# First MLP matrix of a decoder block: squared quarter held on chip, the order of its activation sums, and their layout in memory

## The chip, the cores and the metric

The kernel runs on one core of a Trainium2 chip. The metric is the device time of one execution in microseconds (us), as the median of several runs. Engines are called PE (TensorE), DVE (VectorE), ACT (ScalarE), POOL (GpSimd) and SP (SyncE); the latter two only issue DMAs in the parts that matter here. PSUM is the matmuls' accumulator memory, SBUF the on-chip memory with 128 partitions.

## The reference

A single decoder block in fp32 on 512 tokens of width 2048: RMSNorm, a gated mix of a short convolution and a forgetting attention, a projection back, then an RMSNorm and an MLP with a squared ReLU, and a final RMSNorm. The part that the change touches is the MLP:

```python
h = rmsnorm(x, g_mlp)              # 512 x 2048
u = jnp.square(jax.nn.relu(h @ w_ff1))   # w_ff1 2048 x 8192
x = x + u @ w_ff2                  # w_ff2 8192 x 2048
```

## The kernel before, in words

**Matrix products.** All large products are done in 2 x 2 blocks by a scheme with seven products in place of eight (A11, A12, S4, S2, S3, S1, A22). For each, sums and differences of blocks are formed on both sides: "weight sums" of quarters of w, and "sums of activations". Each fp32 operand is split into a high part that PE multiplies directly (type fp32r) and a low part, the difference: `split` (L99 to L102) writes th on ACT (L101) and tl on DVE (L102). A product is three passes, high by high, high by low, low by high.

**The first MLP matrix** has 16 groups of 512 columns of w_ff1, each one object of the class Group (L166). A group loads four quarters of 1 MB, x00, x10, x01, x11, on SP's queue (L174 to L181), each into a buffer that a done quarter has released (`free`). `head` (L216) runs the products A11 and A12 and hands the quarter (0,0) of the result to `put`; `tail` (L232) runs S4, S2, S3, S1, hands over (1,1) and (0,1), then runs A22 and hands over (1,0). Each product has 48 matmuls of 128 x 256 here. Weight sums are `sub` (L105), four a group; the sums of results are `add` (L108); `snap` (L194) copies a finished accumulator out of PSUM into a small tile o. One product's th and tl have two buffers each.

**After the matrix.** `put_u` (L809 to L847) receives a quarter, applies ReLU in place (L836), squares it (L813), and when both quarters of a column half j are there, forms the seven sums of activations that the second matrix will need: `sums(j)` (L815 to L833) writes them to a tile r of 7 x 256 values per partition, copies the high part to rh (ACT, L829), leaves the low part in r (DVE, L830), and stores both to the DRAM array s_d on POOL's queue (L832 and L833). There is one buffer for r and one for rh. Quarter (0,0) comes long before its partner (1,0), so it is squared at once, stored to the DRAM array c_d (L839, on POOL's queue), and read back into r (L818) when sums(0) is formed.

`sums(0)` is not called at once: `put` appends it to the list `later`, which the next group's `tail` drains after the S4 product (L241). `sums(1)` is called directly by the put of quarter (0,1); quarter (1,0), which completes sums(0), is the last of a group.

**What sets the order.** Engines run their instructions in order, each waiting on semaphores. Tile pools decide when a buffer may be written again: the next r waits until the store of the last one has landed. The framework lays out each engine's order from the written order and may set an instruction ahead of one that it does not depend on.

**The second MLP matrix** goes through w_ff2 in 8 segments. `load_sums` reads the sums of a segment from s_d into tiles us (L872 to L881), three tiles of two sums each and one of a single sum, on POOL's queue; `unit` (L929) loads quarters y of w_ff2 on SP's queue and runs the seven products. The first tile is requested in the last group of the first matrix, the other three behind it. s_d holds, for each partition, seven sums, and in each two parts (high, low), four row blocks and 256 values, so one store writes runs of 256 values (1 KB) that lie 8 KB apart.

Of the kernel before, what the change touches and what calls it, by code (L numbers as in the profile page):

```python
# [8 lines left out]
F32 = mybir.dt.float32  # L9
F32R = mybir.dt.float32r  # L10
BF16 = mybir.dt.bfloat16
AF = mybir.ActivationFunctionType
# [3 lines left out]
P = 128  # L16
S = 512
# [3 lines left out]
HS = S // 2  # L21
# [4 lines left out]
DFF = 4 * D  # L26
# [19 lines left out]
def tile_hybrid_block(ctx: ExitStack, tc, x, g_mix, w_in, b_f, b_gate, conv_w, w_conv_out,  # L46
                      w_attn_out, w_mix_out, g_mlp, w_ff1, w_ff2, g_final, out):
    nc = tc.nc
    x, out = x[0], out[0]
# [5 lines left out]
    main = ctx.enter_context(tc.tile_pool(name="main", bufs=1))  # L55
    pp = ExitStack()
    psum = pp.enter_context(tc.tile_pool(name="psum", bufs=1, space=bass.MemoryType.PSUM, reuse_waits="tile"))
    dram = ctx.enter_context(tc.tile_pool(name="dram", bufs=1, space=bass.MemoryType.DRAM))

    def phase(name):  # L60
        return tc.tile_pool(name=name, bufs=1, reuse_waits="tile")
# [16 lines left out]
    y_d = dram.tile([CT, P, S], F32, name="y_d")  # L78
    a_d = dram.tile([CT, P, S], F32, name="a_d")
    x1_d = dram.tile([NT, P, D], F32, name="x1_d")  # L80
    c_d = [dram.tile([P, 2, HS], F32, name=f"c_d{i}") for i in range(DFF // S)]
    s_d = [dram.tile([P, 7, 2, 4, HS], F32, name=f"s_d{i}") for i in range(DFF // 1024)]


    warm = const.tile([P, 1], F32, name="warm")
# [18 lines left out]
    def sub(out, a, b):  # L104
        nc.vector.tensor_tensor(out=out, in0=a, in1=b, op=ALU.subtract)  # L105

    def add(out, a, b):
        nc.vector.tensor_tensor(out=out, in0=a, in1=b, op=ALU.add)  # L108
# [50 lines left out]
    def moving(t):  # L159

        return lambda q: (t[:, 0, q, :], t[:, 1, q, :])


    free, later = [0, 1, 2, 3], []

    class Group:  # L166
# [65 lines left out]
        def tail(self):  # L232
            if self.at:
                X = self.X
            else:
                X = {(i, 0): self.load(i, 0) for i in range(2)}
            X[0, 1], X[1, 1] = self.load(0, 1), self.load(1, 1)
            a = self.a
            c = self.acc("c")
            self.run(c, "S4", X[1, 1], True)  # L240
            while later:  # L241
                later.pop(0)()
            sub(X[0, 0], X[0, 1], X[0, 0])
            sub(X[0, 1], X[1, 1], X[0, 1])
            sub(X[1, 1], X[1, 1], X[0, 0])
            self.run(a, "S2", X[1, 1], False)
            sub(X[1, 0], X[1, 0], X[1, 1])
            self.done(1, 1)
            s2 = self.snap(a)
            d = self.acc("d")  # L250
            self.run(d, "S3", X[0, 1], True)
            self.done(0, 1)
            d1 = self.snap(d, self.scale)
            self.run(a, "S1", X[0, 0], False)
            self.done(0, 0)
            s4 = self.snap(a, self.scale)
            add(d1, d1, s4)
            self.put(1, 1, d1)
            self.plus(s4, c, self.scale)
            self.put(0, 1, s4)  # L260
            self.run(d, "A22", X[1, 0], False)
            self.done(1, 0)
            self.plus(s2, d)
            self.put(1, 0, s2)
# [55 lines left out]
    def rstd_of(part):  # L320
        v = stat.tile([P, 1], F32, tag="v", name="v")
        nc.vector.tensor_reduce(out=v, in_=part, axis=AX.X, op=ALU.add)
        r = stat.tile([P, 1], F32, tag="r", name="r")
        nc.gpsimd.tensor_tensor(out=r, in0=v, in1=mhalf, op=ALU.pow)
        return r
# [64 lines left out]
    for t in range(NT):  # L390
        h = xp[t // 2][:, t % 2]
        n = 4 if t == 0 else 2
# [182 lines left out]
    n = 0  # L575
# [45 lines left out]
    for c in range(4):  # L621
        held = main.tile([P, 4, S], F32, tag="x1", name="held")
# [183 lines left out]

    def put_u(g):  # L809
        quarters = {}  # L810

        def square(v, out):
            nc.scalar.activation(out=out, in_=v, func=AF.Square)  # L813

        def sums(j):  # L815
            r = pf.tile([P, 7, HS], F32, tag="r", name="r")
            if j == 0:
                nc.gpsimd.dma_start(out=r[:, 0:6:5], in_=c_d[g])  # L818
            else:
                square(quarters[0, j], r[:, 0:6:5])  # L820
            low = quarters[1, j]
            square(low[:, 1, :], r[:, 3, :])
            square(low[:, 0, :], low[:, 0, :])
            add(r[:, 4, :], low[:, 0, :], r[:, 3, :])
            sub(r[:, 1, :], r[:, 0, :], low[:, 0, :])
            sub(r[:, 2, :], r[:, 4, :], r[:, 0, :])
            sub(r[:, 6, :], r[:, 5, :], r[:, 2, :])
            h = pf.tile([P, 7, HS], F32R, tag="rh", name="rh")
            nc.scalar.activation(out=h, in_=r, func=AF.Copy)  # L829
            nc.vector.tensor_tensor(out=r, in0=r, in1=h.bitcast(F32), op=ALU.subtract)  # L830
            q = 2 * (g % 2) + j
            nc.gpsimd.dma_start(out=s_d[g // 2][:, :, 0, q, :], in_=h.bitcast(F32))  # L832
            nc.gpsimd.dma_start(out=s_d[g // 2][:, :, 1, q, :], in_=r)  # L833

        def put(i, j, v):
            nc.scalar.activation(out=v, in_=v, func=AF.Relu, scale=common)  # L836
            if (i, j) == (0, 0):
                square(v, v)
                nc.gpsimd.dma_start(out=c_d[g], in_=v)  # L839
                return  # L840
            quarters[i, j] = v
            if j == 0:
                later.append(lambda: sums(0))
            elif len(quarters) == 2:
                sums(1)

        return put  # L847

    def ff1(g, banks):
        return Group(w_ff1, g * S, g * S + HS, HS, Q2.moving, mm_cols, banks, put_u(g))  # L850
# [3 lines left out]
    pf = ph.enter_context(phase("pf"))  # L854
    n = turns[0] + 1
# [16 lines left out]
    def load_sums(seg, ks, ST):  # L872

        for k in ks:
            place, names = US[k]
            t = main.tile([P, 2, 2, 4, HS], F32R, tag=f"t{place}", name="us")
            nc.gpsimd.dma_start(out=t[:, :len(names)].bitcast(F32), in_=s_d[seg][:, 2 * k:2 * k + len(names)])
            for e, n in enumerate(names):
                ST[n] = moving(t[:, e])

    for g in range(2, DFF // S):  # L881
        group = ff1(g, ((2 + 2 * (g % 2),), (3,), (1,), (7,)))
        group.head(True)
        if g == DFF // S - 1:
            us0 = {}
            load_sums(0, (0,), us0)
        group.tail()

    load_sums(0, (1, 2, 3), us0)
    later.pop()()  # L890
    ph.close()
# [105 lines left out]
    for seg in range(NSEG):  # L997
        ST = us0
        if seg > 0:
            ST = {}  # L1000
            load_sums(seg, range(4), ST)
        if seg == 1:
            gf = pg.tile([P, D], F32, tag="h", name="gf")
            nc.gpsimd.dma_start(out=gf, in_=g_final.partition_broadcast(P))
        for cg in range(2):
            unit(seg, cg, ST)

    for t in (2, 3, 0, 1):
        r = rstd_of(ss3[:, t, :])
# [43 lines left out]
```

## Time and profile before

| | us |
|---|---|
| median of 3 runs | 2546.12 |
| lowest, highest | 2540.99, 2546.52 |
| profiled execution, its time | 2549.66 |
| span of its records | 2547.8 |
| busy: PE, DVE, ACT, POOL | 2469.5, 1904.8, 1144.5, 128.2 |
| mean granted TensorE clock | 0.992 |
| first matrix, 1249 to 1900: PE, DVE, ACT busy of 651 | 620.6, 537.2, 371.7 |
| second matrix, 1900 to 2548: PE, DVE, ACT busy of 648 | 622.6, 526.3, 243.1 |
| 1 MB load of w_ff1, median from issue to landing | 8.4 |
| 896 KB store of rh, of r | 6.4, 7.8 |
| 2 MB load of us | 10.0 |

"Busy" is the time in which an engine executed. A line of the waits names the engine and the line of code that waited, then what released it, then the total, the number of waits and the longest. The chain of waits follows the last instruction back from releaser to releaser. The clock of a stretch is a share of TensorE's full rate.

### The profile page before, as it was taken

To read this page: it belongs to the slowest core of one execution; us is meant where nothing else is said; L and a number is where in the kernel's file an instruction comes from. 1 tells how busy PE (TensorE), PEld (TensorE's weight loads), DVE (VectorE), ACT (ScalarE), POOL (GpSimd) and SP (SyncE) were. 2 spreads that over 40 slices of the span, in tenths; PEclk is the share of its full clock that TensorE was granted. 3 is DMA by queue.
4 is the path that set the end of the run, shared out by engine and by line. 5 is a ranking of instruction groups with operands and counts; after the bars stand their busy time and mean duration, and the time that the engine had idled before them with its cause. 6 is when DMAs were issued, how large, how long until landed. Compare 5 with 4: busy or idle time off the path is not lost.

```text
span 2547.8 us, 39010 instructions
## 1 busy us (share of the span) xinstructions
PE 2469.5 (97%) x16895; PEld 2269.4 (89%) x16895; DVE 1904.8 (75%) x1498; ACT 1144.5 (45%) x1120; POOL 128.2 (5%) x184
## 2 busy tenths in 40 slices
PE   8999999999999999999989999999999999999997
PEld 7999899999999988888889999999998887787785
DVE  7877677779767734435778888888887878878888
ACT  6433443344444622235545655655654333333343
POOL 0000000000000000000001111111111000000000
PEclk9999999999999999999999999999999999999998
DMA  7554444466443544436565665757587556654573
GB/s 240 158 186 153 155 137 129 133 195 210 138 150 115 199 159 143 136 118 231 167 199 182 216 218 189 246 171 236 193 299 286 181 210 219 226 194 162 191 256 106
DMA packets 287871, 473.45 MB, mean 186 GB/s; under 512 B 10236, under 2 KB 194644, under 8 KB 283476
## 3 DMA queue, kind: packets, MB, share of 16 engines
q1 hardware_dynamic: 260704, 330.40, 40.6%
q0 software_dynamic: 26128, 139.47, 14.7%
q8 instruction: 132, 2.16, 0.3%
q10 hardware_dynamic: 868, 1.10, 0.1%
q14 instruction: 39, 0.32, 0.0%
HBM read 374.46 MB, written 96.47 MB: 185 GB/s over the span
## 4 chain that ended last, share of the span: by engine, by line
PE 49%; DVE 12%; DMA 10%; issue 6%; ACT 4%; POOL 1%; POOLq 0%; ACTq 0%; SPq 0%; DVEq 0%
DMA s_d<-r 5%; DVE tl L102 5%; DMA x<-in_w_ff_dram 4%; ACT th L101 4%; PE a L137 3%; PE a L139 3%; PE a L141 3%; PE a L154 3%; PE a L155 2%; PE a L157 2%; PE pt L295 2%; PE pn L304 2%; PE pn L302 2%; PE pt L297 2%; PE pn L303 2%
## 5 line engine op out<-in xcount | busy, mean ns | idle before, releaser
L102 DVE TENSOR_TENSOR tl<-x,th 128x2048 fp32r<-128x2048 f32 (+1 forms) x252 | 576.0, 2289 | 215.0 <-ACT th L101 199.9
L101 ACT ACTIVATE th<-x 128x2048 fp32r<-128x2048 f32 (+1 forms) x252 | 481.8, 1916 | 474.1 <-PE a L139 164.2
L105 DVE TENSOR_TENSOR x<-x,x 128x2048 f32<-128x2048 f32 (+1 forms) x144 | 329.3, 2287 | 32.5 <-DMA x<-in_w_ff_dram 24.8
L101 ACT ACTIVATE th<-y 128x2048 fp32r<-128x2048 f32 x80 | 153.6, 1921 | 270.2 <-DVE y L105 102.9
L102 DVE TENSOR_TENSOR tl<-y,th 128x2048 fp32r<-128x2048 f32 x80 | 182.8, 2285 | 43.6 <-ACT th L101 43.6
L137 PE MATMUL a<-ST,th 128*128 128x256 f32 x768 | 186.1, 286 | 22.6 <-ACT th L101 19.7
L154 PE MATMUL a<-th,us 128*128 128x512 f32 x512 | 201.7, 394 | 4.4 <-ACT o L836 3.4
L102 DVE TENSOR_TENSOR tl<-raw,th 128x2048 fp32r<-128x2048 f32 x40 | 91.7, 2293 | 150.7 <-ACT th L101 150.2
L155 PE MATMUL a<-th,us 128*128 128x512 f32 x512 | 200.1, 391 | 0.0
L139 PE MATMUL a<-ST,th 128*128 128x256 f32 x768 | 184.4, 283 | 0.0
L137 PEld LDWEIGHTS a<-ST,th 128*128 128x128 f32 x768 | 149.7, 195 | 25.4 <-ACT th L101 22.3
L101 ACT ACTIVATE th<-raw 128x2048 fp32r<-128x2048 f32 x40 | 76.7, 1918 | 176.7 <-PE pt L296 71.5
L139 PEld LDWEIGHTS a<-ST,th 128*128 128x128 f32 x768 | 149.7, 195 | 0.0
L137 PE MATMUL a<-S,th 128*128 128x256 f32 x576 | 136.2, 280 | 4.3 <-ACT th L101 4.2
L157 PE MATMUL a<-tl,us 128*128 128x512 f32 x512 | 136.8, 389 | 0.1
L139 PE MATMUL a<-S,th 128*128 128x256 f32 x576 | 135.6, 279 | 0.0
L154 PEld LDWEIGHTS a<-th,us 128*128 128x128 f32 x512 | 96.6, 189 | 29.6 <-ACT th L101 6.2
L137 PE MATMUL d<-ST,th 128*128 128x256 f32 x512 | 118.1, 277 | 1.0 <-ACT o L194 1.0
L139 PE MATMUL d<-ST,th 128*128 128x256 f32 x512 | 118.0, 276 | 0.0
L155 PEld LDWEIGHTS a<-th,us 128*128 128x128 f32 x512 | 96.7, 189 | 19.7
L157 PEld LDWEIGHTS a<-tl,us 128*128 128x128 f32 x512 | 96.0, 188 | 20.4 <-DVE tl L102 0.5
L137 PEld LDWEIGHTS a<-S,th 128*128 128x128 f32 x576 | 108.5, 188 | 5.6 <-ACT th L101 5.3
(276 smaller groups left out, 6257.8 us busy)
## 6 DMA issues: line engine op xcount, KB each, us to landing
x<-in_w_in_dram SPq DMA_DIRECT2D x86, 1024.0 KB, 5.8
x<-in_w_ff_dram SPq DMA_DIRECT2D x66, 1024.0 KB, 8.4
y<-in_w_ff_dram SPq DMA_DIRECT2D x64, 1024.0 KB, 6.2
us<-s_d POOLq DMA_DIRECT2D x24, 2048.0 KB, 10.0
s_d<-rh POOLq DMA_DIRECT2D x32, 896.0 KB, 6.4
s_d<-r POOLq DMA_DIRECT2D x32, 896.0 KB, 7.8
raw<-in_w_mix_out_dram SPq DMA_DIRECT2D x24, 1024.0 KB, 5.1
g_d<-o SPq DMA_DIRECT2D x32, 256.0 KB, 2.2
```

The costliest lines, as they stand in the source:

```text
L101: nc.scalar.activation(out=hi, in_=src, func=AF.Copy)
L102: nc.vector.tensor_tensor(out=lo, in0=src, in1=hi.bitcast(F32), op=ALU.subtract)
L105: nc.vector.tensor_tensor(out=out, in0=a, in1=b, op=ALU.subtract)
L137: nc.tensor.matmul(o, hi[:, q, js], Sh, start=first and q == 0 and j == 0, stop=False, skip_group_check=True)
L139: nc.tensor.matmul(o, hi[:, q, js], Sl, start=False, stop=False, skip_group_check=True)
L141: nc.tensor.matmul(o, lo[:, q, js], Sh, start=False, stop=q == nq - 1, skip_group_check=True)
L154: nc.tensor.matmul(o, Sh, hi[:, q, :], start=begin and q == 0, stop=False, skip_group_check=True)
L155: nc.tensor.matmul(o, Sl, hi[:, q, :], start=False, stop=False, skip_group_check=True)
L157: nc.tensor.matmul(o, Sh, lo[:, q, :], start=False, stop=q == nq - 1, skip_group_check=True)
L295: nc.tensor.matmul(ps[j], hi[:, q, js], xh, start=k == 0, stop=False)
L297: nc.tensor.matmul(ps[j], lo[:, q, js], xh, start=False, stop=k == kt - 1)
L302: nc.tensor.matmul(ps, xh, hi, start=first, stop=False)
```

## The change

Three things in the first matrix, and one line on a bank:

1. c_d is gone. `hold` squares quarter (0,0) into an on-chip tile c (one buffer, 2 KB per partition); sums(0) copies it into r on ACT. `hold` itself goes through `later`.
2. `later` is drained behind the snapshot that follows the S2 product, not behind S4, so that the written order has the weight sums first.
3. s_d has the seven sums innermost: one store writes one run of 7 x 256 values (7 KB) per partition. A tile us is then read in two DMAs (high and low), in runs of two sums, 2 KB (1 KB for the tile with one sum).
4. In the last group the accumulator c of S4 lies in bank 2 and not in bank 1.

```diff
-    c_d = [dram.tile([P, 2, HS], F32, name=f"c_d{i}") for i in range(DFF // S)]
-    s_d = [dram.tile([P, 7, 2, 4, HS], F32, name=f"s_d{i}") for i in range(DFF // 1024)]
+    s_d = [dram.tile([P, 2, 4, 7, HS], F32, name=f"s_d{i}") for i in range(DFF // 1024)]
...
             self.run(c, "S4", X[1, 1], True)
-            while later:
-                later.pop(0)()
             sub(X[0, 0], X[0, 1], X[0, 0])
...
             s2 = self.snap(a)
+            while later:
+                later.pop(0)()
...
+    held = []
...
             if j == 0:
-                nc.gpsimd.dma_start(out=r[:, 0:6:5], in_=c_d[g])
+                nc.scalar.activation(out=r[:, 0:6:5], in_=held.pop(0), func=AF.Copy)
...
-            nc.gpsimd.dma_start(out=s_d[g // 2][:, :, 0, q, :], in_=h.bitcast(F32))
-            nc.gpsimd.dma_start(out=s_d[g // 2][:, :, 1, q, :], in_=r)
+            nc.gpsimd.dma_start(out=s_d[g // 2][:, 0, q], in_=h.bitcast(F32))
+            nc.gpsimd.dma_start(out=s_d[g // 2][:, 1, q], in_=r)
+
+        def hold():
+            c = pf.tile([P, 2, HS], F32, tag="c", name="c")
+            square(quarters[0, 0], c)
+            held.append(c)
 
         def put(i, j, v):
             nc.scalar.activation(out=v, in_=v, func=AF.Relu, scale=common)
+            quarters[i, j] = v
             if (i, j) == (0, 0):
-                square(v, v)
-                nc.gpsimd.dma_start(out=c_d[g], in_=v)
-                return
-            quarters[i, j] = v
-            if j == 0:
+                later.append(hold)
+            elif j == 0:
                 later.append(lambda: sums(0))
-            elif len(quarters) == 2:
+            elif (0, 1) in quarters and (1, 1) in quarters:
                 sums(1)
...
-            t = main.tile([P, 2, 2, 4, HS], F32R, tag=f"t{place}", name="us")
-            nc.gpsimd.dma_start(out=t[:, :len(names)].bitcast(F32), in_=s_d[seg][:, 2 * k:2 * k + len(names)])
+            t = main.tile([P, 2, 4, len(names), HS], F32R, tag=f"t{place}", name="us")
+            for e in range(2):
+                nc.gpsimd.dma_start(out=t[:, e].bitcast(F32), in_=s_d[seg][:, e, :, 2 * k:2 * k + len(names)])
...
-        group = ff1(g, ((2 + 2 * (g % 2),), (3,), (1,), (7,)))
+        group = ff1(g, ((2 + 2 * (g % 2),), (3,), (1 if g < DFF // S - 1 else 2,), (7,)))
```

More of the change, by code (lines that the diff above doesn't have):

```diff
@@ L875, in load_sums @@
             place, names = US[k]
-            t = main.tile([P, 2, 2, 4, HS], F32R, tag=f"t{place}", name="us")
-            nc.gpsimd.dma_start(out=t[:, :len(names)].bitcast(F32), in_=s_d[seg][:, 2 * k:2 * k + len(names)])
+            t = main.tile([P, 2, 4, len(names), HS], F32R, tag=f"t{place}", name="us")
+            for e in range(2):
+                nc.gpsimd.dma_start(out=t[:, e].bitcast(F32), in_=s_d[seg][:, e, :, 2 * k:2 * k + len(names)])
             for e, n in enumerate(names):
-                ST[n] = moving(t[:, e])
+                ST[n] = moving(t[:, :, :, e])
     for g in range(2, DFF // S):
-        group = ff1(g, ((2 + 2 * (g % 2),), (3,), (1,), (7,)))
+        group = ff1(g, ((2 + 2 * (g % 2),), (3,), (1 if g < DFF // S - 1 else 2,), (7,)))
         group.head(True)
```

## The prediction

> **What bounds the kernel now.** I read the page first, then the waits of each engine in the stage of the first MLP matrix, then the chain of waits of one group, then the DMA view of the same stretch.
>
> ```profile
> PE 2469.5 (97%) x16895; PEld 2269.4 (89%) x16895; DVE 1904.8 (75%) x1498; ACT 1144.5 (45%) x1120; POOL 128.2 (5%) x184
> ```
>
> TensorE is nearly always busy, so the change can only win what PE loses now. The table by stage gives for this stage, 1249 to 1900 us of the span:
>
> ```profile
> 1249.00:1900.00 651.00, 620.64 (x5330) 616.88 (x5328) 537.20 (x402) 371.74 (x365) 79.01 (x96) 0.98 0.63 209
> ```
>
> PE is idle 651.0 − 620.6 = 30.4 us there, and runs at a clock of 0.98. For 13 steady groups (1345.8 to 1870.6, each from its S4 product to the next) the period is 524.8 / 13 = 40.37 us. The matmuls of this stage follow each other at 0.1133 us, so a group's 7 × 48 = 336 need 38.08 us. The excess is 2.29 us a group, 29.8 us in all: 17.5 idle (the same table gives 507.3 busy of 524.8), and 12.3 in which PE is busy but slow. Two slices of that table around one stall say where the slow part is from:
>
> ```profile
> 1431.50:1434.40 2.90, 0.82 (x7) 0.63 (x7) 2.90 (x3) 2.13 (x2) 0.00 (x0) 1.00 0.95 325
> 1434.40:1437.80 3.40, 3.40 (x17) 3.40 (x18) 3.11 (x3) 3.24 (x4) 1.29 (x2) 0.50 0.23 65
> ```
>
> A gap of 2.9 − 0.8 = 2.1 us, then 3.4 us at clock 0.50: half of it, 1.7 us, is lost. A larger stall so costs itself and 1.7 us. (The Trainium skill, "TensorE: Matmul & The Clock Gate", Part 1, asks for no PE gaps over some 3.4 us; by that none of these stalls, at most 3.2 us in the steady groups, would halve the clock, and removing them would be worth 17.5 us, not 29.8, and the 21.7 us below would be some 13. The 0.50 behind a gap of 2.1 us speaks against that reading, so the trace's figure stands.)
>
> What makes PE stall, from the waits of all engines in the same stretch:
>
> ```profile
> POOL r L818 <- DMA s_d<-r: 67.7, 14, 6.0
> ACT th L101 <- DVE x L105: 61.2, 14, 4.6
> ...
> ACT r L813 <- DMA s_d<-r: 36.2, 16, 6.5
> ...
> DVE x L105 <- DMA x<-in_w_ff_dram: 24.8, 14, 3.9
> ...
> PE a L137 <- ACT th L101: 19.7, 13, 2.8
> ...
> DVE r L105 <- DMA r<-c_d: 12.1, 6, 4.9
> ```
>
> PE waits once a group (13 times) for th of S2. ACT's th waits for the weight sums on DVE, and DVE for x. The chain of one group names the transfers behind it:
>
> ```profile
> 1671.73 6.32 DMA s_d<-r
> ...
> 1678.33 0.72 POOL r L818
> ...
> 1688.84 11.83 DMA s_d<-r
> ...
> 1700.76 0.07 ACT r L813
> ```
>
> A loop closes on itself. Means of groups 1 to 13, from the timeline: S2's start to the end of tl of S1 (call it T0) 10.0 us; T0 releases the buffer for x01, which lands 11.9 us later, and the store of sums(0) is issued 2.2 us after T0 and lands 13.1 us after it. The next tl of A12 can start 3.8 us after x01 or 2.65 us after that landing, whichever is later (a sum on DVE lies ahead of it, and ACT has r, L813, ahead of its th): 16.4 us after T0. From there DVE and ACT run without a gap to the next S2, 13.9 us. 10.0 + 16.4 + 13.9 = 40.3, the period measured.
>
> **The change, part by part.** *c_d goes.* Per group a 256 KB store and a 256 KB load vanish from POOL's queue, 0.52 MB, 1.4 us of the DMA engines at the 375 GB/s that they reach while crowded, and at a bad place: between T0's predecessors and the loads of x. The r add (L105) no longer waits for c_d: 12.1 us in 6 groups. ACT gets a copy of 128x512 instead, 0.62 us by the square of the same shape (L813), 16 times. It stands ahead of th of S1, where ACT waits about 1 us for PE now, and S1's product starts only some 4 us later, so I cost it at nothing; if that cover is gone it is 16 × 0.62 = 10 us at most.
>
> *The sums move behind tl of S3.* In the built order PE and SP are unchanged. On DVE one add per group moves behind tl of S3; the sums stay ahead of tl of S1. On ACT th of S3 no longer stands behind r (L813), which waits 36.2 us in 16 cases for the store's landing; the copy out of c now meets that wait. Behind it in ACT's queue are r<-o, c<-o, th of S1, rh and the snapshot. In the group at 1677 the landing came at 1678.05 and th of S1 began at 1681.27, held by PE; with 1.66 us of small work in between, 1.6 us of slack stays. Together with c_d I take the first leg from 10.0 to 9.0 us: groups in which c_d was not late show 8.2 to 9.3 now. Bounds: 0 (DVE is late anyway) and −1.8.
>
> *Seven sums in a row.* Each store goes as rows of 7 KB, not 1 KB. In 1693 to 1696 us a store of r crosses a load of x:
>
> ```profile
> q0 software_dynamic: 240, 0.93, 82.3%
> q1 hardware_dynamic: 210, 0.21, 20.7%
> ```
>
> Equal numbers of packets, so the queues alternate packet by packet: 0.823 × 16 × 3 / 240 = 165 ns for 3.9 KB of the store, 47 ns for 1 KB of x. A line through both gives an estimate of 292 ns for 7 KB. A 896 KB store is then 8 packets per DMA engine, 2.3 us, instead of 15, 2.4 us, and lets 7 fewer packets of x through. Two stores: 14 × 47 ns = 0.66 us of x that come behind, not between. So the store lands up to 0.66 + 1.4 us sooner, I take 1.5; x01 is 1.4 sooner for c_d and up to 0.66 later for this, I take 0.75. The second leg's later end gains 1.1: 16.4 to 15.3. Bounds: −2.1, and +0.7 if the rows give no relief and c_d none.
>
> The loop is then 9.0 + 15.3 + 13.9 = 38.2, beside the 38.08 of PE. As legs scatter by about 1 us, and a late group cannot be made up, I take 38.7: 13 × (40.37 − 38.7) = **21.7 us**.
>
> *The first groups.* The longest wait for c_d, 4.9 us, is there: r waits until 1320.5, the store of r is issued at 1326.2 and lands at 1335.9, ACT waits for it, and PE stalls 1.0 and 3.3 us (d, and b L137 <- ACT th L101) with a half-clock stretch behind. Without c_d that store leaves some 4 us sooner. Of 1.0 + 3.3 + 1.7 = 6.0 I take **5 us**.
>
> *Reads for the second matrix.* us is read in 64 DMAs of 2 KB runs, not 32 of 16 KB runs; the total is the same and first use lies 15 us or more behind it, except at the start, where y10's load (21.3 us) runs beside 16 KB packets of 611 ns and costs about 0.6 us of PE. Bounds −1.5 (that stall and a sooner landing) and +3 (a late us at the start, whose k=1 tile has about 2 us to spare); I take **−0.9**. The bank of the last group changes nothing: that first product waits for another bank.
>
> Sum: 21.7 + 5 + 0.9 = 27.6 us of the profiled run's 2549.66 (its span is 2547.8): 2522.1. That run is 3.5 us above the median shown, 2546.12; on the median's scale it is 2518.6. I predict 2520. All excess of these parts gone, 29.8 + 6 + 1.5 = 37.3, gives 2509.
>
> **Rivals.** (a) *Only the wait for c_d goes.* x01 and the stores land no sooner, because stores and loads of x fill the DMA engines anyway (99% busy in slices). For it: x00 and x10 are what c_d collides with, x01 is issued later. Against: c_d<-o landed only at 1686.63, when T0's loads start. Loop 39.3, say 39.5 with scatter: 13 × 0.87 + 5 = 16 us, **2532**. (b) *c_d was covered.* 12.1 us of wait in 6 groups are also taken up by DVE being ahead; the late landing then moves to tl of A12 unchanged: **2543**, within 0.2%. The change also does less than it says on DVE: the sums still precede tl of S1. (c) *Slower: long packets starve x.* With 292 ns against 47, x01 and x11 get 14% of a DMA engine while a store runs, 22% before. If the stores are queued deep ahead of x01, x01 lands after T0 + 13.5 rather than 11.9 and the weight sum on DVE becomes the later end of the second leg; from there every us adds to the period. At 1 us a group it is 13 × 1.0, and 1.7 in some four groups more for the clock: about 20 us, less the 5 at the start: **2561**. Against it: only 0.66 us can be displaced by my count, and c_d's 1.4 us go. (The Trainium skill, "DMA: Bandwidth & Descriptors", Queues, rings and completion order, says that each engine goes round its queues a whole packet at a time; the equal counts above agree.)
>
> **Chances.** Forecast (2509 to 2529) 0.60; (a) 0.17; (b) 0.09; (c) 0.14. About 0.2%, 5 us, is what a measurement of this kernel can tell from no change. Faster 0.77, same 0.09, slower 0.14. The range for 8 in 10 takes the forecast, (a), and the edge of (b): 2508 to 2545.
>
> **What would show it.** No DVE wait for c_d; PE's waits for th of S2 down from 19.7 to under 8 us; period near 38.7; the clock of the stage at 0.99; x01 landing about 11 us after its issue and the store of sums(0) under 12 us after T0; POOL's store issue to landing no longer than now; the b stall of 3.3 us gone. Wrong, if x01 takes longer than 12 us, if ACT waits for s_d before th of S1 and PE's a then waits at S1, or if y and us delay the second matrix by more than 1 us.

## The result and the profile after

The changed kernel takes 2523.35 us in the median of 6 runs (2512.57 to 2533.48), the kernel before 2546.32 (2533.48 to 2551.06). The ratio is 0.9913, with a 95% interval of 0.9891 to 0.9935: 23 us faster, 2520 was forecast. The profiled execution of after took 2533.48 us (span 2531.8), 16.2 less than that of before. Three stages, each from its first matmul to that of the next (the first from the span's start):

| us | before | after | difference |
|---|---|---|---|
| ahead of the first MLP matrix | 1242.3 | 1245.2 | +2.9 |
| first MLP matrix | 660.0 | 643.9 | −16.1 |
| second MLP matrix, to the last matmul | 632.3 | 629.4 | −2.9 |

The first row holds nothing that the change touches; what it shows comes below. The page of after, its engines and the chain that ended last:

```profile
PE 2477.9 (98%) x16895; PEld 2281.2 (90%) x16895; DVE 1901.8 (75%) x1498; ACT 1153.8 (46%) x1136; POOL 112.5 (4%) x184
...
PE 69%; DVE 8%; ACT 3%; DMA 1%; issue 1%; POOL 0%; ACTq 0%; POOLq 0%; SPq 0%; DVEq 0%
```

DMA had been 10% of the chain and DVE 12%; PE is 69% of it now, 49% before. The row of the table by stage for 1249 to 1900 us:

```profile
1249.00:1900.00 651.00, 641.02 (x5402) 637.66 (x5401) 548.72 (x414) 391.42 (x392) 40.27 (x71) 1.00 0.60 205
```

PE is idle 10.0 us in place of 30.4. Its waits in that stretch, all of them, and then three lines from the list of all engines:

```profile
PE a L136 <- ACT th L100: 7.1, 3, 2.7
PE c L136 <- ACT th L100: 1.6, 1, 1.6
PE a L153 <- ACT o L842: 1.2, 1, 1.2
```

```profile
DVE x L104 <- DMA x<-in_w_ff_dram: 5.0, 4, 2.5
...
ACT rh L830 <- DVE r L104: 4.7, 14, 0.7
...
ACT r L814 <- DMA s_d<-r: 4.2, 1, 4.2
```

The 13 waits for th of S2 (in 13 of the 16 groups) are down to 3, all in the first groups. b's stall of 3.3 us is gone, DVE waits 5.0 us for x (24.8 before) and never for c_d, ACT's r waits once. So the loop that the prediction describes no longer holds PE up. Yet the period of the 13 steady groups is 39.78 us, 0.59 less than before, not the 1.67 that was forecast: 12 of them take 39.57 us, without one stall. The matmuls themselves are further apart. The same 35 us of the span in before, another stretch of before, and the first in after (columns: length, PE busy with its number of matmuls, PEld, DVE, ACT, POOL, clock, DMA share, GB/s):

```profile
1476.00:1511.00 35.00, 35.00 (x312) 35.00 (x311) 28.52 (x23) 19.43 (x19) 4.53 (x6) 1.00 0.62 207
1353.00:1388.00 35.00, 35.00 (x299) 35.00 (x298) 27.53 (x23) 20.94 (x22) 3.69 (x5) 1.00 0.58 190
```

```profile
1476.00:1511.00 35.00, 35.00 (x300) 35.00 (x298) 30.22 (x21) 21.52 (x23) 2.13 (x4) 1.00 0.54 194
```

PE is busy throughout and the clock is 1.00 in all three, but 312 matmuls start in the first and 299 or 300 in the others. From start to start it is 113.3 ns or 117.8 ns, with no value between, for a whole stretch: 336 of them make 38.08 or 39.57 us. Before has both, after the slow one from 1350.8 us for 537 us on end. In the 13 steady groups 353 of before's 4368 intervals are slow, and 4319 of after's: against 113.3 ns throughout that is 1.6 us in before and 19.2 in after. This is not in the prediction, and the experiments had to separate it from the loop.

### The profile page after: what moved, and what is told of

The parts are those of the page before. It is cut to its first block, busy times and chain, and to the rows that moved or that the text cites. A ratio compares the mean times of both kernels' runs of the same rounds, so it can differ in the third digit from the quotient of the medians.

```text
span 2531.8 us, 38985 instructions
## 1 busy us (share of the span) xinstructions
PE 2477.9 (98%) x16895; PEld 2281.2 (90%) x16895; DVE 1901.8 (75%) x1498; ACT 1153.8 (46%) x1136; POOL 112.5 (4%) x184
## 4 chain that ended last, share of the span: by engine, by line
PE 69%; DVE 8%; ACT 3%; DMA 1%; issue 1%; POOL 0%; ACTq 0%; POOLq 0%; SPq 0%; DVEq 0%
PE a L136 6%; PE a L138 6%; PE a L140 6%; PE d L138 4%; PE d L136 4%; PE d L140 4%; PE a L153 3%; PE a L154 2%; PE a L156 2%; ACT th L100 2%; DVE tl L101 2%; PE pt L295 2%; PE pt L296 2%; PE pn L302 2%; PE pn L301 2%; PE pn L303 2%
## 5 line engine op out<-in xcount | busy, mean ns | idle before, releaser
L104 DVE TENSOR_TENSOR x<-x,x 128x2048 f32<-128x2048 f32 (+1 forms) x144 | 329.0, 2285 | 11.7 <-DMA x<-in_w_in_dram 6.1
L136 PEld LDWEIGHTS a<-ST,th 128*128 128x128 f32 x768 | 146.3, 190 | 7.7 <-ACT th L100 7.7
L138 PEld LDWEIGHTS a<-ST,th 128*128 128x128 f32 x768 | 146.2, 190 | 0.0
L138 PE MATMUL d<-ST,th 128*128 128x256 f32 x512 | 121.6, 280 | 0.0
L136 PE MATMUL d<-ST,th 128*128 128x256 f32 x512 | 121.6, 280 | 0.0
L156 PEld LDWEIGHTS a<-tl,us 128*128 128x128 f32 x512 | 96.0, 188 | 20.7 <-DVE tl L101 0.9
```

The source lines that it names most:

```text
L136: nc.tensor.matmul(o, hi[:, q, js], Sh, start=first and q == 0 and j == 0, stop=False, skip_group_check=True)
L138: nc.tensor.matmul(o, hi[:, q, js], Sl, start=False, stop=False, skip_group_check=True)
L156: nc.tensor.matmul(o, Sh, lo[:, q, :], start=False, stop=q == nq - 1, skip_group_check=True)
```

## The experiments

Theory: two limits, the loop (forecast at 38.2 us after the change) and PE at one of two spacings. Rivals: the loop is itself 39.57; or the slow spacing is what PE gives without rest. The times of kernels run together share their runs of before.

**The edits by themselves.** hold_only, rows_only and order_only are before with one part of the diff each; hold_order is after with the old layout of s_d.

```diff
hold_only:  -  r[:, 0:6:5] <- DMA of c_d[g]
            +  r[:, 0:6:5] <- copy of held.pop(0); hold() appended to later
rows_only:  -  s_d tile [P, 7, 2, 4, HS]
            +  s_d tile [P, 2, 4, 7, HS]; us read in two DMAs
order_only: -  later drained behind run(c, "S4")
            +  later drained behind s2 = self.snap(a)
```

> Before, with c_d replaced by the on-chip tile c alone (sums still drained behind S4, old layout of s_d). First theory (the loop through c_d, x01 and the store sets the period): no wait of DVE for c_d, first leg about 9.5 instead of 10.0 us, x01 about 0.7 us sooner; PE idle in the 13 steady groups falls from 17.5 to about 8 us, the first groups win 5 us; about -13 us. Rival (c_d was covered): idle stays at 15 to 18 us, time within 0.2%. Cadence theory, found in the trace of after: matmuls of 256 columns follow each other at 113.3 or at 117.8 ns, and keep the one they have until PE next pauses, so a group without a stall takes 38.08 or 39.57 us; the stretches of this kernel show only these two values, and a change of value only behind a pause.

> Before, with the new layout of s_d alone (stores in rows of 7 KB, us read in 64 DMAs; c_d stays). First theory: the store of sums(0) lands 0.5 to 1 us sooner after T0, x01 up to 0.4 us later; PE idle in the steady groups 12 to 17 us; -3 to -6 us in all. Rival (long packets starve x): x01 lands later than 12.5 us after T0, idle rises above 20 us and the time by 10 us or more. Cadence theory: stalls remain, so both cadences appear, with a change behind a stall only.

> Before, with the list of postponed sums drained behind the snapshot of S2 alone (c_d and the old layout stay). First theory: DVE still waits for c_d, th of S3 no longer stands behind the r that waits for the store's landing; first leg 9.6 us, PE idle of the steady groups 14 to 17 us, -2 to -5 us. Rival (it does nothing, since the sums still precede tl of S1): within 0.2%, idle 17 to 18 us.

> After without the new layout of s_d (and without the moved bank): c on chip and the sums drained behind S2. First theory: PE idle of the steady groups about 4 to 6 us, so a period of 38.5 at the quick cadence, and -18 us in all; the difference to after is what the rows of 7 KB bring. Rival (the rows are what matters): idle above 12 us. Cadence theory: where the stalls are gone the period is 38.08 or 39.57, one of them over many groups, and its time lies apart from another run of the same kernel by up to 13 x 1.49 = 19 us for this stage alone.

| | median, us | ratio to before (95%) | first matrix, us | stalls in 13 groups, us | period, us |
|---|---|---|---|---|---|
| before | 2549.5 | 1 | 660.0 | 19.6 | 40.38 |
| hold_only | 2524.63 | 0.9916 (0.9883 to 0.9949) | 643.2 | 2.2 | 39.73 |
| rows_only | 2530.94 | 0.9927 (0.9899 to 0.9954) | 645.8 | 2.9 | 39.78 |
| order_only | 2545.75 | 0.9986 (0.9964 to 1.0008) | 662.1 | 21.8 | 40.44 |
| hold_order | 2530.85 | 0.9917 (0.9887 to 0.9947) | 642.0 | 5.6 | 39.56 |

(The last three columns are of the profiled executions, that of before as in the first table; a stall is what a gap of over 0.3 us between starts of matmuls has beyond one interval. Kernels run later had runs of before of their own, 2545.9 and 2542.31 us in the median, and their ratios go by these.) c on chip and the rows of 7 KB each bring as much as the whole change, and the order brings nothing that can be measured. My figures for single edits failed, for hold_only by size (−13 us expected, −25 in the medians), for rows_only (−3 to −6 expected, −19) by far, and for order_only (−2 to −5 expected), whose interval includes no change. But both kernels show the same picture as after: one stall, then 39.57 us in every group. In hold_order the two limits are seen side by side. Its groups 3 to 6 are at the quick spacing and stall by 0.63, 1.00, 0.96 and 0.43 us; behind the last of these PE goes on at the slow spacing, and the other groups take 39.57 us with no stall. So that loop is about 39 us by these stalls, too long for 38.08 and short enough for 39.57. In order_only DVE still waits for c_d, and PE for th of S2 (from all waits):

```profile
PE a L137 <- ACT th L101: 17.1, 14, 2.3
DVE r L105 <- DMA r<-c_d: 15.6, 7, 4.6
```

**Disturbing the spacing.** One matmul of a product is issued as two of half the columns:

```diff
-   nc.tensor.matmul(o, hi[:, q, js], Sl, start=False, ...)
+   for cs in halves(q, j):   # two slices of 128 columns at q == 4, j == 0
+       nc.tensor.matmul(o[:, cs], hi[:, q, js], Sl[:, cs], start=False, ...)
```

halves7 does it in every 256-column product, halves1 in every seventh, both on after.

> After, with one of the 48 matmuls of every 256-column product issued as two of 128 columns (same sums, same result), so PE's stream is disturbed once a product without any wait. Cadence theory: the disturbance lets the spacing of the matmuls be drawn anew 7 times a group, as a stall does, so both 113.3 and 117.8 ns appear in the stretch from 1350 to 1860 us, changes fall on the split matmuls, and the mean of the steady groups lies between 38.1 and 39.6 us with no 500 us stretch of one value; two halves cost at most 0.01 to 0.1 us more than one whole, 0.1 to 0.7 us a group. Rival 1 (the slow value is what PE gives without rest, whatever the alignment): 117.8 ns throughout, time as after or up to 9 us longer. Rival 2 (halves are dear): period over 40 us.

> The same with one split matmul in every seventh 256-column product only (once a group of the first MLP matrix). Cadence theory: one chance a group to change the spacing; stalls left a quick stretch behind them in some 3 of 4 cases, so the steady groups last 38.1 to 38.6 us after a quick draw and 39.6 after a slow one, the mean over runs 5 to 10 us below after. Rival 1 (rest, not alignment): 117.8 ns throughout, time as after.

halves1 took 2508.7 us (2502.3 to 2509.36), ratio to before 0.9862 (0.983 to 0.9894); halves7 took 2543.49, ratio 1.0005 (0.9985 to 1.0026). At the split the timeline of PE in halves1 reads (start, duration with its overlap, operation, shape, count):

```profile
1383.85 0.33 PE L145 MATMUL a<-ST,th 128*128 128x128 f32 x2
1384.02 0.33 PE L142 MATMUL a<-ST,th 128*128 128x256 f32 x1
1384.19 0.28 PE L145 MATMUL a<-ST,th 128*128 128x256 f32 x1
```

From the start of the first half to that of the second whole matmul behind is 0.34 us, three times 113 ns: the split costs one more interval, 0.113 us. And it does more than draw anew, which the cadence theory had not expected. I count, from 480 to 1915 us, what lies between one stretch of at least 10 matmuls at one spacing and the next. In the five kernels that split every seventh product, a split with no stretch at half clock beside it led from the slow spacing to the quick one in 20 of 20 cases, and from the quick one it never left it (103 of 103). A pause without a split or half clock (13 kernels, all but halves7) led from quick to slow in 40 of 113 cases, from slow to quick in 17 of 34. So all steady groups of halves1 but the first run at 38.21 us without a stall, and the spread of its runs shrinks from 21 us to 7; the median is 15 us below after, where 5 to 10 were expected. The rival of "rest" falls: 0.1 us without any wait is enough. halves7 is at the quick spacing too, but has 204 more splits, 23 of the 35 us by which it is slower; the other 12 us (7 ahead of the first matrix, 5 behind it) were not followed up.

The stage ahead of the first matrix, 480 to 880 us, has the same 256-column products: 400 us of after at the slow spacing, and in hold_only quick. The same 60 us in after and in hold_only:

```profile
700.00:760.00 60.00, 60.00 (x512) 60.00 (x511) 40.38 (x22) 27.33 (x26) 0.00 (x0) 1.00 0.44 132
```

```profile
700.00:760.00 60.00, 60.00 (x531) 60.00 (x531) 39.33 (x22) 28.77 (x29) 0.00 (x0) 1.00 0.53 162
```

It is why the first row of the first table moves by itself: 1245.2 us in after, 1229.0 in hold_only. Before ran a fifth of these matmuls (675 intervals) at the quick spacing, which is the 3 us by which its first row is shorter than after's.

**How long is the loop after the change?** more_dve adds 1.26 us of DVE work to every group of after; hold_rows is after without the moved drain and bank.

```diff
more_dve:  -  sub(r[:, 6, :], r[:, 5, :], r[:, 2, :])
           +  the same four times for j == 0
```

> After, with the last of the sums(0) formed four times instead of once (1.26 us more on DVE in every group, ahead of tl of S1; the result is the same). Cadence theory: at the slow spacing PE needs 39.57 us a group and the loop through DVE and the loads is shorter, about 38.2 to 38.7 us, so the loop becomes 39.5 to 40 and costs at most 0 to 6 us in 13 groups. Rival (39.57 is the loop itself, the new period is set by DVE and the transfers): 13 x 1.26 = 16 us more and a stall in every group.

> After without the moved drain and the moved bank (c on chip, rows of 7 KB, sums drained behind S4). First theory, as amended by the single edits (each of c on chip and rows of 7 KB alone already brings the loop below the 39.57 us that PE needs at the slow spacing): no stalls in the slow stretches, time equal to after within the scatter of single runs, 2515 to 2535 us. Rival (the order matters once the other two are there): stalls at S2 of 0.5 us or more in most groups and 5 us more than after.

more_dve took 2526.17 us, ratio 0.9916 (0.9885 to 0.9948); its profiled execution fell on the quick spacing (that of after on the slow one), and

```profile
1476.00:1511.00 35.00, 35.00 (x312) 35.00 (x311) 31.95 (x27) 20.97 (x22) 1.60 (x3) 1.00 0.57 205
```

it runs 12 groups on end at 38.08 us (one of them 38.19) without a stall, 1.26 us notwithstanding. Not all of the 1.26 us is in the loop's way: in halves1 DVE has 0.28 us to wait in front of this tl, and the shortest first legs (S2 to T0) are 9.2 us in more_dve and 8.2 in halves1. So the loop of after is at most 38.08 − 1.0 = 37.1 us, shorter than the 38.2 forecast and than my 38.2 to 38.7 in the expectation, and 39.57 was PE, not the loop. The rival falls. hold_rows took 2515.16 us, ratio 0.9899 (0.9867 to 0.9931), first matrix 643.8 us, as after (643.9): the order adds nothing there either.

**The parts with the spacing held.** The split of halves1 in before, and in before with one or two parts of the change:

> Before, with the split matmul in every seventh 256-column product, which holds the spacing of the matmuls at 113.3 ns, so that stalls alone are left. Amended theory (two limits: a loop of about 40.3 us through c_d, the stores and x01, and PE's 38.08 or 39.57): the loop binds, so the first MLP matrix stays within 5 us of before (653 us from its first to the last matmul) with a period of 40 us; only the stage ahead of it, 480 to 880 us, gains up to 15 us. Rival (the spacing alone was the change's gain): the first MLP matrix drops below 640 us.

> The tile c on chip in place of c_d alone, at the quick spacing. Amended theory: the loop without c_d is about 39 us (hold_order showed stalls of 0.6 to 1.0 us in its quick groups), above 38.2: stalls of 0.5 to 1 us in most groups, first MLP matrix 620 to 633 us. Rival (c_d was the whole loop): no stalls, as halves1.

> The rows of 7 KB alone, c_d kept, at the quick spacing. Amended theory: the loop is below 39.57 us (rows_only had no stall at the slow spacing) but above 38.2, so stalls of 0.3 to 1 us in most groups, first MLP matrix 620 to 633 us, and DVE still waits for c_d. Rival (the rows are the whole gain): no stalls in the steady groups, as halves1.

> Both, without the moved drain and bank, at the quick spacing. Amended theory: the loop is about 37 us, below PE's 38.2; no stalls, first MLP matrix within 3 us of halves1, so the moved drain brings nothing that counts. Rival (the order is needed): stalls of 0.3 us or more in most groups.

| with the split | median, us | ratio to before (95%) | first matrix | stalls in 13 groups | period |
|---|---|---|---|---|---|
| before | 2536.96 | 0.9967 (0.9945 to 0.999) | 656.9 | 20.3 | 40.30 |
| c on chip | 2518.62 | 0.989 (0.9856 to 0.9924) | 638.9 | 12.2 | 39.41 |
| rows of 7 KB | 2519.18 | 0.9891 (0.9858 to 0.9924) | 638.9 | 6.1 | 39.03 |
| both | 2507.89 | 0.9843 (0.9806 to 0.988) | 628.6 | 3.2 | 38.49 |
| all (halves1) | 2508.7 | 0.9862 (0.983 to 0.9894) | 627.0 | 2.4 | 38.43 |

Here the parts add in good part: in the first matrix each brings 18 us and both together 28, where PE's floor cuts them off; at the slow spacing one part alone had brought as much as all. The split alone leaves before's first matrix where it was, so the loop bound there, and moves the time by the stage ahead. The first matrix came out at 638.9 where 620 to 633 was expected of either part: the stalls of the first groups remain. PE's waits for th of S2 in before, with c on chip, with the rows, and with both, all with the split:

```profile
PE a L143 <- ACT th L101: 19.5, 10, 2.9
```

```profile
PE a L142 <- ACT th L100: 15.6, 14, 2.9
```

```profile
PE a L143 <- ACT th L101: 8.1, 7, 2.8
```

```profile
PE a L142 <- ACT th L100: 4.9, 3, 2.7
```

The legs of the loop, means of groups 1 to 13 as in the prediction (x01, store and tl of A12 count from T0):

| us | S2 to T0 | x01 lands | store lands | tl of A12 | then to S2 |
|---|---|---|---|---|---|
| before | 10.0 | 11.7 | 13.1 | 16.3 | 14.0 |
| before with the split (before_halves) | 9.7 | 11.5 | 13.2 | 16.2 | 14.2 |
| c on chip (hold_halves) | 8.9 | 12.2 | 13.6 | 16.5 | 13.9 |
| rows (rows_halves) | 8.9 | 11.7 | 11.1 | 15.7 | 14.3 |
| all (halves1) | 8.2 | 11.0 | 11.1 | 15.1 | 14.9, PE's turn |

c on chip shortens the first leg only. The rows shorten both: the store lands 2.1 us sooner, x01 becomes the later end of the second leg, and DVE's waits for c_d fall from 8.4 to 4.8 us. That these fall because a store that lands sooner lets the read of c_d start sooner is argued, not shown. The store itself is faster where no load runs beside it, in the issues of the DMA view, 1710.9 to 1718.6 us of before and 1698.6 to 1704.9 us of after:

```profile
s_d<-rh POOLq DMA_DIRECT2D x1, 896.0 KB, 4.7
s_d<-r POOLq DMA_DIRECT2D x1, 896.0 KB, 5.3
```

```profile
s_d<-rh POOLq DMA_DIRECT2D x1, 896.0 KB, 3.9
s_d<-r POOLq DMA_DIRECT2D x1, 896.0 KB, 3.9
```

These are typical: 30 such stores of after have a median of 3.9 us, 29 of before one of 5.3. Beside loads (13 stores of rh in each) the larger difference is at the start: from the issue to the first packet it takes 4.6 us in the median of before, 2.7 in hold_only, 1.1 in rows_only and in after. The store of r behind it then lands 13.2 us after the issue of rh in before and 11.9 in rows_only and after, so most of that head start is lost again on the way.

And packets beside a load, with a store under way all the time (after, 1682.5 to 1684.5 us):

```profile
q0 software_dynamic: 101, 0.72, 85.8%
q1 hardware_dynamic: 112, 0.10, 17.3%
```

## Why the prediction came out, point by point

**The bound.** Right: the loop held PE, and it was the loop that the change shortened. The floor beneath it was the step that failed: "a group's 7 × 48 = 336 need 38.08 us". That is one of two values. The rows of before already had the other, 299 matmuls in 35 us at clock 1.00, and I put all of the slow busy time down to the clock. For before that was nearly right: of its excess of 29.8 us, 19.6 are stalls, 8.1 half clock and 1.6 the slow spacing. For after it was not: 19.2 of its 22.2 us are the slow spacing.

**First leg, 10.0 to 9.0.** Right in kind; 8.9 by c on chip alone, 8.2 in all. The copy on ACT shows no cost, as forecast. The moved sums were given a share of it and have none that shows: order_only is 0.9986 (0.9964 to 1.0008), and hold_rows equals after. The rows were given none and have one: 8.9 by the rows alone.

**Second leg, 16.4 to 15.3.** Measured 15.1, but the parts are not those of the sum. The 1.4 us of traffic that c_d takes away brought x01 and the store nothing by itself (12.2 and 13.6 us with c on chip, 11.5 and 13.2 before, all with the split): of this, rival (a) was right. On top of the rows it goes with an x01 that lands 0.7 us sooner (11.0 against 11.7). The rows alone brought the store forward by 2.1 us, where 0.66 was the most that I allowed them. I had priced a store by the time of its packets, 2.3 against 2.4 us of the DMA engines. Alone the packets take 279 ns for 7 KB and 189 ns for 4 KB, 2.23 against 2.65 us a store, and I left out what lies ahead of them: POOL's issue (0.53 in place of 0.94 us) and the wait for the first packet.

**Long packets starve x.** Rival (c) did not come in the time, though its mechanism is there. In the rows above, 101 packets of the store went beside 112 of x, at 272 ns and 49 ns (292 and 47 in the estimate), and x has 17.3% of the engines, 20.7% in the prediction's rows of before. Over all half microseconds of the steady groups in which stores had over 60% of the engines, the counts are 4906 to 4871 in before and 1889 to 2346 in after. (The Trainium skill, "DMA: Bandwidth & Descriptors", Queues, rings and completion order, has each engine drain a whole packet before the next queue's turn; these nearly equal counts agree.) But x01 lands 11.7 us after T0 with the rows alone, 11.5 without them, and not 13.5 as in the rival.

**The sum.** 21.7 us were forecast of the steady groups. With the spacing held they give 13 × (40.30 − 38.43) = 24.3. In the profiled pair they give 13 × 0.59 = 7.7 only: stalls and half clock fall by 24.7 us, and the slow spacing takes 17.6 back. The rest of the stage, mostly the first groups, gave 16.1 − 7.7 = 8.4 (5 forecast), the second matrix 2.9 (0.9 forecast): the wait at its start fell from 3.4 to 1.2 us, in hold_only as well, so the bank has no part in it. That the median, −23 us, came near the 27.6 of the working is partly luck: a loop that became shorter than forecast and a floor that was higher worked against each other, and the stage ahead, which the change doesn't touch, differs by 16 us between profiled executions with its spacing.

**What is open.** What sets the two spacings, and why a split leads to the quick one. What holds back the first packet of a store in rows of 1 KB while loads run. And how much of the scatter of the medians is this: only profiled executions show the spacing.

## What to carry to other kernels

When PE is near its bound, count matmuls over stretches without a stall, at several places, before taking one spacing as the floor: here 4% lay between two values at the same clock. A change that takes a loop below that floor shows no more than the floor allows, so single edits look as good as all of them together; hold the floor fixed to see what each is worth. And time a store from its issue to its landing, alone and beside loads, before you price it by its packets: here 3.5 us of difference beside loads lay ahead of the first one.

## What the runs showed of the hardware

- Matmuls of 256 columns followed each other at 113.3 or 117.8 ns with PE busy and the clock at 1.00, and kept the value for up to 537 us, until a stall, a stretch at half clock or a split. The last two mostly led to the quick one: 20 of 21 stretches at half clock without a split, and 123 of 123 splits without half clock (13 traces, 480 to 1915 us).
- Two matmuls of 128 columns in place of one of 256 cost 0.113 us. One in 336 removed the slow spacing: after with that split is 2508.7 us, the fastest form of the changed kernel, and its runs lie within 7 us. With the drain and bank of before it took 2507.89, which is no measurable difference.
- A store of 896 KB in 128 rows of 7 KB landed in 3.9 us alone, in rows of 1 KB in 4.7 to 5.3; its issue on POOL took 0.53 us in place of 0.94. Beside loads its first packet came 1.1 us after the issue in place of 4.6.
- With a store and loads under way together, the two queues moved about as many packets each: 240 to 210 with packets of 4 KB against 1 KB, 101 to 112 with 7 KB against 1 KB.
